# Moving a conditioning gate's row sums out of the seam between attention and output projection, and pacing an MLP between half products

## The chip, the cores and the metric

One core of a Trainium2 chip runs the whole program. The metric is the device time of one execution in microseconds. The kernel before took 890.24 us (median of 3 runs, 889.83 to 891.96). All matrix products run on TensorE (PE). VectorE (DVE), ScalarE (ACT) and GpSimd (POOL) do the elementwise work, and SyncE (SP) issues nearly all transfers.

## The reference

One decoder layer for 1024 tokens and a model width of 1024. All of this is computed in float32:

- `mod = c @ w_ada + b_ada` gives a shift, a scale and a gate of 1024 numbers each, from one conditioning vector `c`.
- `h = rms_norm(x) * (1 + scale) + shift`, and `proj = h @ w_in` gives queries, keys, values, SiLU gate paths (z) and merge gates.
- Mixer A is sparse attention with 8 heads in 2 groups: a compressed branch, whose keys and values come from blocks of 32 tokens through a small MLP (2048 to 256 to 64), a branch over selected blocks, and a window of 512. Mixer B is attention over a window of 128, with sinks, also 8 heads in 2 groups.
- Both outputs are multiplied with `silu(z)`, projected, merged with `sigmoid(m_a)` and `sigmoid(m_b)`, and multiplied by `w_out`.
- The result is `x + gate * rms_norm(y)`. The gate is the last third of `mod`, and nothing needs it before this last line.

With 16 blocks of 64 tokens and 16 to select, every causal block is selected, so the kernel does that branch as full causal attention.

## The kernel before

**Precision.** Each product of two float32 matrices is made from a high and a low part of each operand: high by high, high by low and low by high, three matmuls into the same PSUM bank. So every weight block is first *split*: a copy to the high type on ACT (L179, or L175 on DVE for two of them, or L177) and a subtraction on POOL (L182). Activations are split on ACT and DVE.

**Stages, in order of time in the profile.**

1. Up to about 60 us: `mod` for shift and scale (multiply-and-reduce on DVE over rows of `w_adaT`, L290), the norm, h for the first half of the tokens, and the first products.
2. About 60 to 166 us: h for the second half of the tokens, the values' products, and then two things in parallel: the products for six gate blocks Z (`z_halves`, lines 588 to 593, each block in two halves of the tokens, 24 matmuls of 512 columns each), and the compression MLP (`mlp`, lines 641 to 696), once for keys (side 0) and once for values (side 1). The MLP loads eight slices of `w1` per side, splits each on ACT (L653) and DVE (L654) and multiplies it in six matmuls of 256 columns (L657 to L659). POOL meanwhile forms sums of h (`input_sums`, from line 724), tied to marks among the Z products (`z_marks`). These sums are for a fast matrix product (seven half-size products in place of eight) that computes most of the merge gates.
3. About 166 to 696 us: four attention units, (B,0), (B,1), (A,0) and (A,1). Each goes over 8 blocks of 128 queries. For each head: scores on PE (L864, L867), adding the distances and taking the minimum on DVE (L874), the exponential on ACT (L887), the scale on POOL (L896), a transpose on PE (L933), its split on ACT and DVE (L939, L940), and the products with the values (L941, L944). Between these, projections fill PE (`b_pj`, L205 to L213 in the first two units, L1004 to L1010 in the last two).
4. About 691 to 809 us, the seam and the output: the last parts of the fast merge gate product (L1341 to L1345), loading the heads' outputs back and splitting them (`heads_out`, L1325 to L1327), the projections of the heads (`gated`, L1401 to L1403), and sums of `w_out` rows for the fast product with `w_out`.
5. To the end: that product (L1531 to L1536), norm, gate and addition.

**What sets the order.** The program is traced in Python, and a planner then puts every engine's instructions in an order: it simulates a timeline, takes the instruction with the highest priority of those that are ready, and takes tile buffers from a free pool. Each engine runs its own queue in that order, and SP's queue holds nearly all transfers. `tc.high_priority(offset=n)` moves a block forward or, with a negative offset, back. `after(a, b)` and `chain(tag, a)` add a dependency without a semaphore: it orders the plan, and between instructions of one engine it orders their queue. The clock of the plan inside the units is `done[0]`, which counts attention columns only: `mark` appends a score or transpose matmul to `marks`, `held(at)` returns the matmul that was there at that time, and `AHEAD = 3` is how much earlier than its place a thing may go. `pieces` is a list of (time, function); `pump` calls those that are due, at low priority. In the units before the change, only (A,0) and (A,1) use it.

**Places that the change touches.**

- Gate rows. `gate_load` (from line 1352) loads 8 row blocks of `w_adaT` of 128x1024, 512 KB each, in the seam, and L1374 loads `c` broadcast to all 128 rows. `gate_sum` (from line 1357) multiplies and reduces on DVE, L1359. They use the places of the heads' tiles `oh0` to `oh3`, `ol0` and `ol1`.
- Key fronts. `k_block` puts 64 columns of compressed keys ahead of each half of the keys of the selected branch, L543 (high) and L544 (low), on DVE, into a tile of the tag `kts`.
- `set_form` (L1058 to L1063) splits the sums of h for the fast product, a copy on ACT and a subtraction on POOL, when a projection piece begins (`Part.piece`). There `hold[0] = held(at - AHEAD)` stood after the call that triggers these copies.

The tag `kts` has 8 buffers, which the MLP's `w1` parts, the key tiles and the sums of weight quarters (`paced_sums`) share.

## Time and profile before

| What | Value |
|---|---|
| Median of 3 runs | 890.24 us |
| The profiled execution | 895.18 us |
| Span of that execution, first to last instruction | 893.3 us |
| Granted TensorE clock, mean | 0.988 |
| Busy: PE, DVE, ACT, POOL | 868.8, 630.2, 534.1, 532.7 us |
| Moved by DMA | 151.46 MB, 170 GB/s mean |

"Busy" counts the time in which an engine executes an instruction. Matmuls overlap in a pipeline: a 512-column matmul is listed with some 0.39 us, but in a full stream a new one starts each 0.23 us. So a busy PE can still be slow, and the number of matmuls in a stretch says more than its busy time. A row of the groups of instructions is: line, engine, operation, the tile written and the tiles read, shapes, count, then times. In a row of the timeline, the bracket at the end is how long the engine had been idle and what ended that. The granted clock is the share of full speed that the throttle let TensorE have.

### The profile page before, as it was taken

What the parts mean: (1) busy time and instruction counts of PE and PEld (TensorE: products, weight loads), DVE (VectorE), ACT (ScalarE), POOL (GpSimd) and SP (SyncE); (2) the same over time, 40 slices, a digit from 0 to 9 for tenths busy, and PEclk for the clock granted to TensorE, in tenths of its full rate; (3) what the DMA queues carried; (4) which work ended last, traced back from release to release, by engine and by line L of the source; (5) the groups of instructions that cost most, each with busy time, mean ns of one, the idle gap of its engine ahead of it and who ended that gap; (6) DMA issues with size and microseconds to landing.
All of it is one profiled execution on the core that took longest, in us unless ns stands there. A gap on an engine that the chain in (4) does not pass through costs nothing.

```text
span 893.3 us, 14739 instructions
## 1 busy us (share of the span) xinstructions
PE 868.8 (97%) x4418; PEld 730.1 (82%) x4418; DVE 630.2 (71%) x1579; ACT 534.1 (60%) x1210; POOL 532.7 (60%) x547
## 2 busy tenths in 40 slices
PE   8999999999999999999999999999999989999996
PEld 6989878888888887878888878888887868887885
DVE  4866775465666577667666677677675499998996
ACT  6466742276777777647657786666565435544341
POOL 1000966867867888866637686654573349855541
PEclk7999999999999999999999999999999989999998
DMA  9875565854534554643333334333553698951323
GB/s 349 282 271 181 178 202 189 287 163 152 180 110 133 171 152 159 212 147 94 99 109 101 89 107 131 107 121 103 163 174 101 243 387 275 331 157 49 107 94 118
DMA packets 92001, 151.46 MB, mean 170 GB/s; under 512 B 10769, under 2 KB 28561, under 8 KB 91922
## 3 DMA queue, kind: packets, MB, share of 16 engines
q1 hardware_dynamic: 90768, 149.30, 50.9%
q10 hardware_dynamic: 1154, 1.23, 0.5%
q8 instruction: 35, 0.57, 0.3%
q14 instruction: 44, 0.36, 0.1%
HBM read 108.81 MB, written 38.01 MB: 164 GB/s over the span
## 4 chain that ended last, share of the span: by engine, by line
PE 82%; DMA 5%; DVE 4%; issue 3%; ACT 2%; POOL 2%; SPq 1%; DVEq 0%; POOLq 0%; ACTq 0%
PE b_pt L933 7%; PE b_pj L1004 6%; PE b_pj L1010 6%; PE b_pj L1009 6%; PE b_pv L944 4%; PE b_s L867 4%; PE b_pj L212 4%; PE b_pj L213 4%; PE b_pj L205 4%; PE b_s L864 4%; PE b_pv L941 4%; DMA wg<-in_w_adaT 2%; PE b_s L228 1%; PE b_s L229 1%; DVE w L654 1%
## 5 line engine op out<-in xcount | busy, mean ns | idle before, releaser
L182 POOL TENSOR_TENSOR wl<-wraw,wh 128x512 fp32r<-128x512 f32 x123 | 167.0, 1361 | 80.7 <-ACT wh L179 61.4
L940 DVE TENSOR_TENSOR pl<-b_pt,ph 128x512 fp32r<-128x512 f32 x162 | 110.6, 687 | 44.0 <-ACT ph L939 41.2
L939 ACT CAST ph<-b_pt 128x512 fp32r<-128x512 f32 x162 | 93.4, 584 | 56.2 <-PE b_pt L933 50.2
L887 ACT ACTIVATE ps<-ps,mins 128x257 f32<-128x257 f32 (+9 forms) x128 | 81.3, 636 | 34.8 <-DVE mins L874 32.4
L179 ACT CAST wh<-wraw 128x512 fp32r<-128x512 f32 x115 | 70.6, 618 | 50.1 <-PE b_pj L1009 19.7
L864 PE MATMUL b_s<-kh,q 128*128 128x256 f32 (+6 forms) x272 | 85.6, 321 | 2.2 <-DVE mins L874 1.7
L867 PE MATMUL b_s<-kl,q 128*128 128x256 f32 (+6 forms) x272 | 83.5, 314 | 0.0
L1004 PE MATMUL b_pj<-hh,wh 128*128 128x512 f32 x188 | 77.7, 413 | 0.0
L896 POOL TENSOR_SCALAR ps<-ps,rr,gates 128x128 f32<-128x128 f32 (+7 forms) x64 | 52.5, 824 | 41.3 <-DVE rr L891 22.2
L1010 PE MATMUL b_pj<-hh,wl 128*128 128x512 f32 x188 | 74.5, 396 | 0.0
L1009 PE MATMUL b_pj<-hl,wh 128*128 128x512 f32 x188 | 74.0, 393 | 0.0
L944 PE MATMUL b_pv<-pl,V 128*128 128x512 f32 x162 | 68.3, 422 | 1.4 <-DVE pl L940 1.2
L941 PE MATMUL b_pv<-ph,V 128*128 128x512 f32 x162 | 67.0, 413 | 2.2 <-DVE ot L958 1.5
L933 PE MATMUL b_pt<-ident,ps 128*128 128x128 f32 x408 | 67.0, 272 | 0.1
L205 PE MATMUL b_pj<-hh,wh 128*128 128x512 f32 x160 | 63.1, 394 | 0.0
L213 PE MATMUL b_pj<-hh,wl 128*128 128x512 f32 x160 | 63.0, 394 | 0.0
L212 PE MATMUL b_pj<-hl,wh 128*128 128x512 f32 x160 | 62.9, 393 | 0.0
L864 PEld LDWEIGHTS b_s<-kh,q 128*128 128x128 f32 x272 | 51.2, 188 | 10.6 <-DVE mins L874 2.6
L933 PEld LDWEIGHTS b_pt<-ident,ps 128*128 128x128 f32 x408 | 51.1, 140 | 10.0 <-DVE pl L940 0.5
L896 POOL TENSOR_SCALAR pw<-pw,rr,gates 128x640 f32<-128x640 f32 (+4 forms) x64 | 47.4, 745 | 19.4 <-DVE rr L891 17.1
L867 PEld LDWEIGHTS b_s<-kl,q 128*128 128x128 f32 x272 | 51.1, 189 | 7.4
L887 ACT ACTIVATE pw<-pw,mins 128x640 f32<-128x640 f32 (+4 forms) x64 | 44.5, 695 | 18.0 <-DVE mins L874 17.8
(453 smaller groups left out, 2502.8 us busy)
## 6 DMA issues: line engine op xcount, KB each, us to landing
wraw<-in_w_blk SPq DMA_DIRECT2D x83, 256.0 KB, 3.2
r<-in_w_out SPq DMA_DIRECT2D x32, 256.0 KB, 5.0
wa<-in_w_adaT SPq DMA_DIRECT2D x15, 512.0 KB, 5.1
wraw<-sS SPq DMA_DIRECT2D x28, 256.0 KB, 2.9
w1raw<-in_w SPq DMA_DIRECT2D x16, 256.0 KB, 4.1
wraw<-in_w_o SPq DMA_DIRECT2D x16, 256.0 KB, 5.0
t<-od SPq DMA_DIRECT2D x16, 256.0 KB, 5.8
wg<-in_w_adaT SPq DMA_DIRECT2D x8, 512.0 KB, 7.0
```

The source lines that it names most:

```text
L182: chain("wl", nc.gpsimd.tensor_tensor(wl, raw, wh.bitcast(F32), ALU.subtract))
L864: ins = nc.tensor.matmul(sp[:, :n_in], lhsT=q, rhs=rh, start=True, stop=False)
L867: nc.tensor.matmul(sp[:, :n_in], lhsT=q, rhs=rl, start=False, stop=True)
L887: nc.scalar.activation(rows[r][:, :on], rows[r][:, :on], AF.Exp, scale=-1.0, bias=last_min[:, r : r + 1], accum_out=sums[:, r : r + 1])
L896: nc.gpsimd.tensor_scalar(rows[r][:, :off], rows[r][:, :off], rr[:, r : r + 1], gate, ALU.mult, ALU.mult)
L933: ins = nc.tensor.transpose(t[:, r * P : r * P + P], rows[r][:, off : off + P], ident)
L940: nc.vector.tensor_tensor(pl, t, ph.bitcast(F32), ALU.subtract)
L941: ins = nc.tensor.matmul(pv, lhsT=v, rhs=ph, start=(first and n == 0), stop=False)
L944: nc.tensor.matmul(pv, lhsT=v, rhs=pl, start=False, stop=(last and n == len(todo) - 1))
L1004: ins = nc.tensor.matmul(self.t, lhsT=wh[:, kc, :], rhs=hi, start=(self.first is None and kc == 0), stop=False)
L1009: nc.tensor.matmul(self.t, lhsT=wh[:, kc, :], rhs=lo, start=False, stop=False)
L1010: ins = nc.tensor.matmul(self.t, lhsT=wl[:, kc, :], rhs=hi, start=False, stop=(kc == KH - 1 and self.stop))
```

## The change

Four edits:

1. **Gate sums.** The loads and sums for the gate leave the seam. Each of the 8 row blocks is halved by columns. Half 0 of all is loaded and summed in unit (B,0), half 1 in unit (B,1), which adds to the first half's partial sum. The halves go through single `kts` buffers (128x512), their half of `c` through a tile of the tag `zt` or `ot`, which the first two units do not use. Loads stand at shares 0.08 + 0.11 k of the unit and sums at 0.14 + 0.11 k, by `pieces`.
2. **MLP between half products.** `z_halves` becomes `z_steps`, which stops in the middle of each product (after 4 of 8 row blocks, 12 matmuls) and at its end. Three steps come before the MLP. Within each side of the MLP, one step follows each of the first seven `w1` slices, at a priority 500 lower, and the first matmul of each next slice is tied behind it. The remaining steps come after. A block's successor is loaded after its first half, and `z_marks` are now the middles of the products.
3. **Key fronts.** The two copies in `k_block` go from DVE to ACT.
4. **Splits tied to half products.** `hold[0]` is set before what begins with a piece, the copies of `set_form` are tied behind `hold[0]`, and the loads of `paced_sums` behind `held` of their own time.

```diff
             elif pre:
-                nc.vector.tensor_copy(khp[:, pre - 64 : pre], kc2[:, 0, keys[r][1], :].bitcast(F32))
-                nc.vector.tensor_copy(klp[:, pre - 64 : pre], kc2[:, 1, keys[r][1], :].bitcast(F32))
+                nc.scalar.copy(khp[:, pre - 64 : pre], kc2[:, 0, keys[r][1], :].bitcast(F32))
+                nc.scalar.copy(klp[:, pre - 64 : pre], kc2[:, 1, keys[r][1], :].bitcast(F32))
...
-    def z_halves(names):
-        for name in names:
-            w = load_block(name)
+    def z_steps(names):
+        w = load_block(names[0])
+        for n, name in enumerate(names):
             for half in range(2):
-                z_block(name, half, w)
-                yield
+                t = bank(("s", "pj")[z_count[0] % 2])
+                for kc in range(KC):
+                    wh, wl = (x[:, kc % KH, :] for x in w[kc // KH])
+                    ins = nc.tensor.matmul(t, lhsT=wh, rhs=hh[kc][half], start=(kc == 0), stop=False)
+                    if kc == 0:
+                        chain("pj", ins)
+                    nc.tensor.matmul(t, lhsT=wh, rhs=hl[kc][half], start=False, stop=False)
+                    ins = nc.tensor.matmul(t, lhsT=wl, rhs=hh[kc][half], start=False, stop=(kc == KC - 1))
+                    if kc == 3:
+                        yield ins
+                z_out(name, half, t)
+                if half == 0 and n + 1 < len(names):
+                    following = load_block(names[n + 1])
+                yield ins
+            w = following
...
-                    nc.tensor.matmul(t[:, :256], lhsT=fh[:, l, :], rhs=h, start=(l == 0), stop=False)
+                    ins = nc.tensor.matmul(t[:, :256], lhsT=fh[:, l, :], rhs=h, start=(l == 0), stop=False)
+                    if n and l == 2 * n:
+                        after(ins, z_done[-1])
...
+                if n < 7:
+                    with tc.high_priority(offset=-500):
+                        z_done.append(next(zs))
...
-        zs = z_halves([f"Z{m}{b}" for m, b in (("B", 0), ("B", 1), ("B", 2), ("B", 3), ("A", 0), ("A", 1))])
+        zs = z_steps([f"Z{m}{b}" for m, b in (("B", 0), ("B", 1), ("B", 2), ("B", 3), ("A", 0), ("A", 1))])
+        z_done = []
+        for _ in range(3):
+            z_done.append(next(zs))
         with tc.high_priority(offset=500):
             blocks_of(0)
             mlp(0)
             blocks_of(1)
             mlp(1)
-        z_marks = []
-        for _ in zs:
-            z_marks.append(last["pj"])
+        z_done += list(zs)
+        z_marks = z_done[::2]
...
+                hold[0] = held(at - AHEAD)
                 if self.before:
                     self.before()
...
-            nc.scalar.copy(hi, lo.bitcast(F32))
+            after(nc.scalar.copy(hi, lo.bitcast(F32)), hold[0])
...
+    gate_c, gate_part = [None], sm.tile([P, 8], F32, name="gpart")
+
+    def gate_half(h):
+        gate_c[0] = at.tile([P, HS], F32, name="cg", tag=("zt", "ot")[h], bufs=1)
+        nc.sync.dma_start(gate_c[0], io["c"][h * HS : h * HS + HS].partition_broadcast(P))
+
+    def gate_sum(k, h):
+
+        blk, part, was = 16 + k, gate_part[:, k : k + 1], []
+
+        def get(when):
+            was.append(kq.tile([P, P + HS], F32, name="wg", tag="kts", bufs=8)[:, :HS])
+            after(nc.sync.dma_start(was[0], io["w_adaT"][blk * P : blk * P + P, h * HS : h * HS + HS]), held(when))
+
+        def add(when):
+            wa = was[0]
+            after(nc.vector.tensor_tensor_reduce(
+                out=wa, in0=wa, in1=gate_c[0], scale=1.0, scalar=part if h else smalls[:, 8 + blk : 9 + blk],
+                op0=ALU.mult, op1=ALU.add, accum_out=mod[:, blk : blk + 1] if h else part), held(when))
+
+        return get, add
...
+            gate_half(u)
+            for k in range(8):
+                for f, share in zip(gate_sum(k, u), (0.08, 0.14)):
+                    pieces.append((begun + whole[u] * (share + 0.11 * k), f))
+            pieces.sort(key=lambda x: x[0])
...
-        gate_c = op.tile([P, S], F32, name="cg", tag="oh0")
-        places = ["oh1", "oh2", "oh3", "ol0", "ol1"]
-        owing = []
-
-        def gate_load(k):
-            wa = op.tile([P, S], F32, name="wg", tag=places[k % 5])
-            nc.sync.dma_start(wa, io["w_adaT"][(16 + k) * P : (17 + k) * P, :])
-            owing.append((16 + k, wa))
-
-        def gate_sum():
-            blk, wa = owing.pop(0)
-            nc.vector.tensor_tensor_reduce(
-                out=wa, in0=wa, in1=gate_c, scale=1.0, scalar=smalls[:, 8 + blk : 9 + blk],
-                op0=ALU.mult, op1=ALU.add, accum_out=mod[:, blk : blk + 1])
...
-            if n == 0:
-                nc.sync.dma_start(gate_c, io["c"].partition_broadcast(P))
-            gate_load(2 * n)
-            gate_load(2 * n + 1)
...
-            if n:
-                gate_sum()
...
-        while owing:
-            gate_sum()
```

More of the change, by code (lines that the diff above doesn't have):

```diff
@@ L557, in k_fills @@
         return [lambda: k_block([("slc", g), ("win", g)], half, load_block(f"KA{g}"))]
-    def z_block(name, half, w):
-        z_out(name, half, proj_half(w, half, lambda: bank(("s", "pj")[z_count[0] % 2])))
     z_count = [0]
@@ L575, in z_out @@
         nc.sync.dma_start(spilled[name][:, half * HS : half * HS + HS], sp)
-    def z_fills(mixer, g):
-        res = []
-        for p in range(2):
-            def block(name=f"Z{mixer}{2 * g + p}"):
-                w = load_block(name)
-                for half in range(2):
-                    z_block(name, half, w)
-            res.append(block)
-        return res
-    def z_halves(names):
-        for name in names:
-            w = load_block(name)
-            for half in range(2):
-                z_block(name, half, w)
-                yield
+    def z_steps(names):
+        w = load_block(names[0])
+        for n, name in enumerate(names):
+            for half in range(2):
+                t = bank(("s", "pj")[z_count[0] % 2])
[13 more added lines that the diff above has]
+            w = following
     spilled = {}
@@ L1179, in paced_sums @@
         quads = {}
-        def get():
+        def get(when):
             a11, a12 = (kq.tile([P, HS], F32, name="sa", tag="kts", bufs=8) for _ in range(2))
@@ L1185, in get @@
             for n, t in ((2, a21), (3, a22), (0, a11), (1, a12)):
-                nc.sync.dma_start(t.rearrange("p (k t) -> p k t", k=KH), quarter_of(PAIRS[p][n // 2], n % 2))
-        return get, lambda: pair_sums(p, *quads[0])
+                after(nc.sync.dma_start(t.rearrange("p (k t) -> p k t", k=KH), quarter_of(PAIRS[p][n // 2], n % 2)),
+                      held(when))
+        return get, lambda when: pair_sums(p, *quads[0])
+    gate_c, gate_part = [None], sm.tile([P, 8], F32, name="gpart")
[4 more added lines that the diff above has]
+        blk, part, was = 16 + k, gate_part[:, k : k + 1], []
+        def get(when):
+            was.append(kq.tile([P, P + HS], F32, name="wg", tag="kts", bufs=8)[:, :HS])
[6 more added lines that the diff above has]
+        return get, add
     late = []
@@ L1241, in hybrid_kernel @@
                     ahead_of(line[k - 2], lambda k=k: set_form("T2", (k,)))
-                def paced(share, f):
-                    pieces.append((begun + whole[u] * share, lambda at: f()))
                 for n, p in enumerate(range(FIRST, NP)):
                     for f, share in zip(paced_sums(p), (0.18, 0.23)):
-                        paced(share + 0.09 * n, f)
+                        pieces.append((begun + whole[u] * (share + 0.09 * n), f))
             else:
@@ L1385, in hybrid_kernel @@
             nc.scalar.activation(y, y, AF.Sigmoid)
-            if n:
-                gate_sum()
             early[b, 1], early[b, 0] = e, y
-        while owing:
-            gate_sum()
         nc.vector.tensor_tensor(amod, mod[:, 16:24], g_post, ALU.mult)
```

## The prediction

> **What bounds the kernel now.** I read first the page's busy times and its chain of waits, to see which engine sets the end:
>
> ```profile
> span 893.3 us, 14739 instructions
> PE 868.8 (97%) x4418; PEld 730.1 (82%) x4418; DVE 630.2 (71%) x1579; ACT 534.1 (60%) x1210; POOL 532.7 (60%) x547
> ...
> PE 82%; DMA 5%; DVE 4%; issue 3%; ACT 2%; POOL 2%; SPq 1%; DVEq 0%; POOLq 0%; ACTq 0%
> PE b_pt L933 7%; PE b_pj L1004 6%; PE b_pj L1010 6%; PE b_pj L1009 6%; PE b_pv L944 4%; PE b_s L867 4%; PE b_pj L212 4%; PE b_pj L213 4%; PE b_pj L205 4%; PE b_s L864 4%; PE b_pv L941 4%; DMA wg<-in_w_adaT 2%; PE b_s L228 1%; PE b_s L229 1%; DVE w L654 1%
> ```
>
> TensorE is idle for only 893.3 - 868.8 = 24.5 us, so a gain can come only from that idle time and from slow matmuls. The change adds and removes no matmul. Yet two things that the change moves stand in the chain by name: wg, the gate rows' load (2% is some 18 us), and w L654, the low half of the compression MLP's weights. Where the idle time lies, the busy times by stretch show (columns: length, PE, PEld, DVE, ACT, POOL busy with instruction counts, granted clock, DMA share, GB/s):
>
> ```profile
> 100.00:125.00 25.00, 22.78 (x119) 18.66 (x118) 20.12 (x17) 15.35 (x22) 19.07 (x13) 1.00 0.59 190
> 725.00:750.00 25.00, 21.46 (x79) 16.52 (x79) 24.39 (x26) 12.39 (x23) 19.42 (x14) 0.86 0.89 311
> 750.00:775.00 25.00, 25.00 (x111) 20.57 (x110) 21.14 (x23) 14.27 (x27) 22.31 (x15) 1.00 0.96 325
> 875.00:893.30 18.30, 10.44 (x58) 8.95 (x56) 11.84 (x24) 2.97 (x10) 1.41 (x2) 0.86 0.27 100
> ```
>
> The tail's 7.9 us is not touched. The worst stretch in reach is 725 to 750: 79 matmuls where the next stretch has 111, DVE busy 24.39 of 25, the clock down to 0.86. At 25 / 111 = 0.225 us each, 32 missing matmuls are 7.2 us. What TensorE waits for, over the whole run (total us, times, longest):
>
> ```profile
> PE b_pt L658 <- DVE w L654: 2.6, 4, 0.7
> PE b_pt L1401 <- ACT oh L1326: 1.8, 1, 1.8
> ...
> PE b_s L864 <- DVE mins L874: 1.7, 1, 1.7
> PE b_pv L941 <- DVE ot L958: 1.5, 2, 1.1
> PE b_pv L944 <- DVE pl L940: 1.2, 4, 0.5
> PE b_pt L1401 <- ACT wh L179: 1.1, 1, 1.1
> ...
> PE b_pt L1402 <- DVE ol L1327: 0.6, 1, 0.6
> ```
>
> So there are three places: the MLP (L658), one stall in the attention (L864), and the seam between attention and output (the L1401 and L1402 rows).
>
> **Part 1, the gate sums leave the seam.** Around 710 the DMA engines are full, and after the first stall the clock is halved:
>
> ```profile
> 710.00:715.00 5.00, 5.00 (x24) 4.14 (x23) 5.00 (x9) 2.50 (x4) 0.00 (x0) 1.00 1.05 415
> ...
> 730.00:735.00 5.00, 5.00 (x14) 3.84 (x14) 4.42 (x7) 1.14 (x2) 3.72 (x3) 0.55 1.03 395
> ```
>
> ```profile
> 727.05 0.50 PE L1401 MATMUL b_pt<-oh,wh 128*128 128x512 f32 x1 [1.83 <-ACT oh L1326]
> ...
> 728.78 0.80 PE L1402 MATMUL b_pt<-ol,wh 128*128 128x512 f32 x1 [0.59 <-DVE ol L1327]
> ...
> 729.80 0.63 PE L1402 MATMUL b_s<-ol,wh 128*128 128x512 f32 x1
> ...
> 734.06 0.60 PE L1403 MATMUL b_pv<-oh,wl 128*128 128x512 f32 x1
> ```
>
> From 729.80 to 734.06 there are ten steps of 0.426 us, 0.20 more than 0.225: idle 1.83 + 0.59 + 1.12 = 3.5 us and slow matmuls 14 x 0.20 = 2.8 us, with the refill of the pipeline after each gap (some 0.2 us each) 7.0 us, which agrees with 7.2 by counting. The transfers behind it:
>
> ```profile
> t<-od SPq DMA_DIRECT2D x16, 256.0 KB, 5.8
> wg<-in_w_adaT SPq DMA_DIRECT2D x8, 512.0 KB, 7.0
> ```
>
> ```profile
> wraw<-in_w_blk SPq DMA_DIRECT2D x83, 256.0 KB, 3.2
> ...
> L1359 DVE CUSTOM_DVE_ANT_0 wg<-wg,cg,smalls x8: 1272/1280/2023, 709.7 to 737.0; 128x1024 f32<-128x1024 f32 x8
> ```
>
> Eight loads of 0.52 MB and the broadcast of c to 128 rows of 4 KB, 4.7 MB in all, are 11.7 us of transfer at about 400 GB/s. They stand on SP's queue between the heads' loads (t), which take 5.8 us to land where a load of the same size takes 3.2 us elsewhere. The first stall waits for such a head. With the gate loads gone the heads' backlog goes, and DVE loses 10.8 us of sums (8 x 1.28, one at 2.02) in the stage where it is full. What is late next: DVE's head splits and the w_out sums, now with 11 us of room between 705 and 760. I take back 6.3 of the 7.0 us, leaving one pipeline gap of 0.7; bounds 7.2 (all) and 3.0 (the clock's 2.8 us and the 0.2 of its refill only, idle stays).
>
> In the Trainium skill, "TensorE: Matmul & The Clock Gate", Part 1, an idle window of about 3.4 us halves the clock. The trace halves it after 1.83 us with 0.59 us behind it, and doesn't at the 1.7 us stall of L864 (clock 1.00, row below). By the page as by these rows, a single short stall that stays would not bring the slow 2.8 us back.
>
> **Part 2, the gate sums enter the first two units.** They become 16 loads of 256 KB, 2 broadcasts of 256 KB and 16 sums of 128x512. The nearest rows for such a sum: the same kind of instruction on 512 columns, and subtractions with both inputs in SBUF beside a busy POOL (min/median/max ns):
>
> ```profile
> L874 DVE CUSTOM_DVE_ANT_0 ps<-b_s,DC 128x512 f32<-128x512 f32 x32 | 21.7, 687 | 5.9 <-PE b_pt L933 4.4 <-PE b_s L867 1.2
> ...
> L654 DVE TENSOR_TENSOR w<-w1raw,w x16: 679/1252/1792, 86.2 to 145.0; 128x512 fp32r<-128x512 f32 x16
> ```
>
> So 0.69 to 1.79 us each, 11 to 29 us in all. What hides them (a sum over 166 to 310, then the low parts of the probabilities and the products that read them, 175 to 310; the loads that mark the two units; the transfers of 160 to 320):
>
> ```profile
> sum 144.00, PE 144.00 PEld 122.48 DVE 87.27 ACT 101.33 POOL 109.03; mean PE 20.57 PEld 17.50 DVE 12.47 ACT 14.48 POOL 15.58
> ```
>
> ```profile
> L940 DVE TENSOR_TENSOR pl<-b_pt,ph x31: 671/685/692, 180.9 to 304.3; 128x512 fp32r<-128x512 f32 x31
> ...
> L944 PE MATMUL b_pv<-pl,V x31: 388/393/483, 185.8 to 306.5; 128*128 128x512 f32 x31
> ```
>
> ```profile
> L955 SPq DMA_DIRECT2D zb<-sp_ZB x32: 592/600/673, 162.0 to 295.0; - x32
> ```
>
> ```profile
> DMA packets 21011, 26.48 MB, mean 166 GB/s; under 512 B 2398, under 2 KB 11358, under 8 KB 20995
> ```
>
> DVE is free for 144 - 87.3 = 57 us there and TensorE never waits. Pairing the 31 low parts with their products in order, the first is ready 4.2 us ahead (180.9 + 0.69 to 185.8), the last, already in the third unit, 1.5 us; of the others none is under 3.1 us. A sum of up to 1.8 us fits under that. Behind each sum on DVE stand score minima and low parts, and TensorE waits for those; behind each load on SP stand weights and spilled tiles, for which nothing waited here. 4.7 MB over the two units' 133 us is 35 GB/s on top of 166, where the seam moved 400. I take 0; bounds -0.3 and +3 (two stalls of the size at L864).
>
> The skill's "SBUF — State Buffer", Who interferes with whom, speaks against this move: a DVE instruction with two SBUF inputs and a GpSimd one that reads SBUF shut each other out for a whole instruction. L654's 1792 ns and L1359's 2023 ns agree. By that rule 16 sums would be near 30 us instead of 11; both are under the 57 us and the 3.1 us of cover, so the sum stays.
>
> **Part 3, the MLP between half products.** Each pair of w1 slices (six matmuls of 0.12 us) now comes after a half of a gate product (twelve of 0.225, 2.7 us). DVE's split, up to 1.79 us, has 3.4 us, so the 2.6 us wait goes. What it adds is alternating. The 256-column matmul ahead of a 512-column one held TensorE for 0.22 us in one place and 0.12 in another:
>
> ```profile
> 112.60 0.38 PE L657 MATMUL b_pt<-w,fh 128*128 128x256 f32 x1
> 112.82 0.40 PE L205 MATMUL b_s<-hh,wh 128*128 128x512 f32 x1
> ```
>
> ```profile
> 142.32 0.28 PE L657 MATMUL b_pt<-w,fh 128*128 128x256 f32 x1
> 142.44 0.40 PE L205 MATMUL b_s<-hh,wh 128*128 128x512 f32 x1
> ```
>
> Some ten more alternations than now: 0 to 1.0 us; I take 0.5, the middle. Net -2.1; bounds -2.6 and +1 (one new wait of 1 to 2 us when the second MLP starts and its flat split is late). The next block's load is issued half a block earlier, and the marks for the sums of h move by some 1.5 us; their product is read 300 us later:
>
> ```profile
> L740 POOL TENSOR_TENSOR q<-hh,hl x8: 1282/1292/3316, 94.4 to 157.9; 128x512 f32<-128x512 f32 x8
> ...
> L1062 ACT CAST hht<-hlt x16: 606/620/627, 463.8 to 656.0; 128x512 fp32r<-128x512 f32 x16
> ```
>
> **Part 4, front copies and split ties.** One front copy is behind the 1.7 us stall at 399: DVE stood 3.23 us before it and then 2.21 us in it, with the score minima queued behind:
>
> ```profile
> 398.60 2.21 DVE L543 CAST kh<-kc 128x64 fp32r<-128x64 f32 x1 [3.23 <-POOL sa L718]
> ...
> 400.00:405.00 5.00, 3.74 (x18) 3.08 (x19) 3.38 (x14) 3.70 (x13) 3.23 (x7) 1.00 0.18 57
> ```
>
> On ScalarE the copy may wait for the same buffer, and then the exponentials and high parts stand behind it. I take half, -0.8; bounds -1.7 and +1.5 (the stall comes back on ACT). Tying the set splits to an earlier mark moves sixteen copies of 0.62 us on ACT within slack: 0, bounds -0.7 and +0.7.
>
> **The sum.** The profiled execution took 895.18 us (span 893.3 and 1.9 around it). -6.3 + 0 - 2.1 - 0.8 = -9.2, so 886.0 us for an execution like it. The median of the runs is 890.24, 4.9 us under the profiled one; the same difference gives 881.0 us. The costs' bounds taken together where most of them are independent give 877 to 885 for this case.
>
> **The rivals.**
> *The seam refills* (0.15). Its stall is not the gate loads' but DVE's and the heads' own: three t buffers, and DVE at 24.39 of 25. For it: the 1.1 us stall waits for a weight split behind w_out sums on DVE. Against: 11 of its busy us are the gate sums. Only 3.0 of 7.0 come back: 881.0 + 3.3 = 884.3.
> *The order in the third and fourth unit gets worse* (0.10). The order is planned anew, and cover is thin there: L864, L941 and L944 wait 1.7 + 1.5 + 1.2 = 4.4 us now. Twice that, and Part 4's gain gone: 881.0 + 4.4 + 0.8 = 886.2. Against: those units get no new work but four pairs of short copies.
> *The half-product order doesn't hold the pairs apart* (0.08): a tie orders the plan, and the splits still come late, 881.0 + 2.1 = 883.1. Against: both are TensorE's, one queue.
> *Slower: each gate sum stops DVE's queue in the first two units* (0.07), waiting for its transfer and for POOL. DVE runs in order, so a block of b us costs 16 x (b - 4.3) once it is over the typical lead, 4.3 us (the pairs above lie between 3.1 and 5.8, but for the last); at b = 5.3, 16 us, so 897. It decides from the point where a load lands 3 us after its plan. For it: 256 KB take 3.2 us to land, and a load stands only 0.06 of a unit (133 / 2 x 0.06 = 4 us) ahead of its sum. Against: being 3 us late needs a landing of 7 us, seen only in the full seam.
>
> **How the numbers follow.** The forecast has 0.60, 877 to 885. Faster or slower by 0.3% (2.7 us) is about what a measurement can tell from no change. Faster (under 887.6): nearly all of the forecast, 0.59, of the seam rival 0.13, of the order rival 0.06, of the MLP rival 0.07, together 0.85; same 0.08, mostly the order rival; slower 0.07. The range 875.5 to 888 takes in the first three rivals and the bounds, and leaves out the slower one and the tails.
>
> **What would show it.** No wg row after 700; 725 to 750 shifted forward with 110 matmuls per 25 us and clock 1.00; t landing near 4 us. L658 without its wait on w. No TensorE wait between 175 and 300, and gate sums of 0.7 to 1.8 us there. The stall at L864 gone or under 1 us, without a new one behind ACT kh. I am wrong if waits on ps, pl or mins appear in the first two units, or if TensorE still stops for oh at the seam.

## The result and the profile after

The changed kernel took 895.04 us (median of 5 runs, 893.19 to 897.33), the kernel before 890.24. The ratio is 1.0053, with a 95% interval of 1.003 to 1.0076: slower by about half a per cent, where 881.0 was forecast. The profiled execution took 896.8 us. Its page begins with the same TensorE time as before:

```profile
span 895.0 us, 14786 instructions
...
PE 870.6 (97%) x4418; PEld 732.0 (82%) x4418; DVE 624.2 (70%) x1587; ACT 534.3 (60%) x1218; POOL 535.9 (60%) x547
...
PE b_pj L1010 7%; PE b_pj L1016 7%; PE b_pj L1015 7%; PE b_pt L938 6%; PE b_pv L949 4%; PE b_s L872 3%; PE b_s L869 3%; PE b_pv L946 3%; POOL hlw L1429 2%; POOL wl L182 1%; PE b_s L1542 1%; PE b_s L1540 1%; PE b_s L1537 1%; PE b_pv L921 1%; POOL wt L1429 1%
```

Both names that the change was to take off the chain, wg and the low half of the MLP's weights, are gone from it, but the time is not shorter. The busy times by stretch show where it went (columns as before). After the change:

```profile
100.00:125.00 25.00, 24.68 (x129) 20.85 (x128) 17.87 (x16) 13.46 (x21) 20.15 (x13) 1.00 0.58 199
...
175.00:200.00 25.00, 20.69 (x90) 16.31 (x89) 8.08 (x30) 10.27 (x29) 9.16 (x11) 0.86 0.71 221
200.00:225.00 25.00, 21.44 (x111) 17.71 (x109) 16.84 (x49) 14.78 (x43) 20.46 (x26) 0.93 0.58 184
225.00:250.00 25.00, 23.76 (x131) 19.86 (x132) 18.71 (x58) 18.33 (x55) 19.55 (x24) 1.00 0.64 190
...
725.00:750.00 25.00, 25.00 (x112) 20.68 (x111) 23.74 (x22) 15.28 (x29) 25.00 (x17) 1.00 0.88 297
```

The same stretches of the two first units before, which the prediction had not shown because nothing waited there:

```profile
175.00:200.00 25.00, 25.00 (x133) 21.25 (x132) 15.58 (x40) 17.26 (x46) 16.20 (x21) 1.00 0.55 171
200.00:225.00 25.00, 25.00 (x135) 21.26 (x134) 14.42 (x43) 17.56 (x48) 18.98 (x24) 1.00 0.53 164
225.00:250.00 25.00, 25.00 (x137) 21.27 (x135) 15.27 (x45) 18.60 (x53) 22.75 (x27) 1.00 0.55 172
```

From 100 to 125 us TensorE is now nearly gapless, and from 725 to 750 it does 112 matmuls in place of 79, at full clock. Both gains came. Between 175 and 225 us it does 201 matmuls in place of 268, with the clock down to 0.86 and 0.93. What TensorE waits for, over the run after:

```profile
PE b_s L869 <- DVE mins L879: 6.0, 4, 2.6
PE b_pt L938 <- POOL ps L901: 2.5, 1, 2.5
PE b_pv L949 <- DVE pl L945: 1.8, 4, 1.1
...
PE b_pt L938 <- DVE pl L945: 1.2, 3, 0.8
```

These are waits on mins, ps and pl, most of them in the first two units (of the 6.0 us on mins, 1.1 stand at 319 us, behind them): what the prediction named as the sign that it is wrong.

To add up slow matmuls and gaps together I use one measure below, the *excess*: the time from each matmul's start to the next one's, less its time in a full stream (0.227 us for 512 columns, in proportion for fewer, 0.085 for a transposition), summed over a stretch. It is good to some 2 us over a whole run.

| Excess, us | before | after | change |
|---|---|---|---|
| MLPs, 100 to 150 | 5.5 | 1.6 | -3.9 |
| first two units, 150 to 300 | 6.8 | 22.4 | +15.6 |
| last two units, 300 to 675 | 31.6 | 26.6 | -5.0 |
| seam, 675 to 775 | 9.7 | 3.2 | -6.5 |

So 15.4 us came and 15.6 went. The two profiled executions lie 1.6 us apart (895.18 and 896.8), the medians 4.8: the profiled execution before was itself 4.9 us above its median, the one after 1.8. A difference between two profiles can therefore be some 3 us off from the difference of the medians. Two places hold most of the 15.6. The first is the start of the first unit (timeline after):

```profile
177.48 0.67 PE L689 MATMUL b_pt<-w2v,h1T 128*63 128x64 f32 x8
...
179.10 0.49 DVE L699 TENSOR_TENSOR vc<-vcf,vc 128x128 fp32r<-128x128 f32 x2
...
179.55 0.34 ACTq L760 DMA_DIRECT2D DC<-in_DC  x1
...
186.35 0.35 DVE L879 CUSTOM_DVE_ANT_0 ps<-b_s,DC,nsink 128x128 f32<-128x128 f32 x1 [3.84 <-DMA DC<-in_DC]
...
186.77 0.33 PE L869 MATMUL b_s<-kh,q 128*128 128x128 f32 x1 [1.82 <-DVE mins L879]
...
190.65 0.47 PE L938 MATMUL b_pt<-ident,ps 128*128 128x128 f32 x1 [2.49 <-POOL ps L901]
...
191.35 0.63 PE L212 MATMUL b_pj<-hl,wh 128*128 128x512 f32 x1
```

The second MLP's last product (w2v) stands at 177.48 us. Then the load of the distance table DC is issued, it takes 6.8 us to land (3.7 before), and only then can the first row of scores be reduced. Before the change the same three steps were:

```profile
160.29 0.33 ACTq L755 DMA_DIRECT2D DC<-in_DC  x1
...
161.08 0.67 PE L686 MATMUL b_pt<-w2v,h1T 128*63 128x64 f32 x8
...
166.94 0.35 DVE L874 CUSTOM_DVE_ANT_0 ps<-b_s,DC,nsink 128x128 f32<-128x128 f32 x1
```

The paced MLP ends 16.4 us later, the table's load starts 19 us later, and TensorE, which had gate products to do until then, has nothing left. The second place is a gate sum (timeline after):

```profile
205.75 0.59 SPq L1209 DMA_DIRECT2D wg<-in_w_adaT  x1
...
209.24 1.77 DVE L1213 CUSTOM_DVE_ANT_0 wg<-wg,cg,smalls 128x512 f32<-128x512 f32 x1 [1.10 <-DMA wg<-in_w_adaT]
...
211.48 0.38 PE L869 MATMUL b_s<-kh,q 128*128 128x256 f32 x1 [2.64 <-DVE mins L879]
...
213.08 0.63 PE L946 MATMUL b_pv<-ph,V 128*128 128x512 f32 x1
```

DVE stands 1.10 us for the load, sums for 1.77 us, and the score minima behind it come 2.64 us too late. Over the run the sums wait for their loads seven times:

```profile
L1213 DVE CUSTOM_DVE_ANT_0 wg<-wg,cg,smalls x8: 739/750/1767, 202.1 to 243.2; 128x512 f32<-128x512 f32 x8
...
  DMA wg<-in_w_adaT: 9.8, 7
```

### The profile page after: what moved, and what is told of

Read it like the earlier page. It is cut to its first block, busy times and chain, and to the rows that moved or that the text cites. A ratio compares the mean times of both kernels' runs of the same rounds, so it can differ in the third digit from the quotient of the medians.

```text
span 895.0 us, 14786 instructions
## 1 busy us (share of the span) xinstructions
PE 870.6 (97%) x4418; PEld 732.0 (82%) x4418; DVE 624.2 (70%) x1587; ACT 534.3 (60%) x1218; POOL 535.9 (60%) x547
## 4 chain that ended last, share of the span: by engine, by line
PE 50%; POOL 4%; issue 3%; DMA 2%; DVE 2%; ACT 1%; SPq 0%; DVEq 0%; POOLq 0%; ACTq 0%
PE b_pj L1010 7%; PE b_pj L1016 7%; PE b_pj L1015 7%; PE b_pt L938 6%; PE b_pv L949 4%; PE b_s L872 3%; PE b_s L869 3%; PE b_pv L946 3%; POOL hlw L1429 2%; POOL wl L182 1%; PE b_s L1542 1%; PE b_s L1540 1%; PE b_s L1537 1%; PE b_pv L921 1%; POOL wt L1429 1%
## 5 line engine op out<-in xcount | busy, mean ns | idle before, releaser
L1010 PE MATMUL b_pj<-hh,wh 128*128 128x512 f32 x188 | 77.4, 412 | 0.0
L1016 PE MATMUL b_pj<-hh,wl 128*128 128x512 f32 x188 | 74.2, 395 | 0.0
L1015 PE MATMUL b_pj<-hl,wh 128*128 128x512 f32 x188 | 73.9, 393 | 0.0
L896 DVE RECIPROCAL rr<-sums 128x1 f32<-128x1 f32 x192 | 28.1, 158 | 27.9 <-ACT pw L892 13.7
L205 PE MATMUL b_pj<-hh,wh 128*128 128x512 f32 x112 | 45.5, 406 | 0.0
L212 PE MATMUL b_pj<-hl,wh 128*128 128x512 f32 x112 | 45.0, 402 | 0.0
```

The costliest lines, as they stand in the source:

```text
L1010: ins = nc.tensor.matmul(self.t, lhsT=wh[:, kc, :], rhs=hi, start=(self.first is None and kc == 0), stop=False)
L1015: nc.tensor.matmul(self.t, lhsT=wh[:, kc, :], rhs=lo, start=False, stop=False)
L1016: ins = nc.tensor.matmul(self.t, lhsT=wl[:, kc, :], rhs=hi, start=False, stop=(kc == KH - 1 and self.stop))
```

## The experiments

Each ratio is to the kernel before, run beside it on the same chip; the chips differ from group to group, so kernels of different groups are compared by their ratios. The "ties" are the two lines `if n and l == 2 * n: after(ins, z_done[-1])`, which put each MLP block behind a half product.

### Taking the parts apart

Four kernels, each the kernel before with some of the four edits:

```
e1_no_mlp     front copies + ties of the splits + gate sums      (MLPs as before)
e2_no_gate    front copies + ties of the splits + paced MLPs     (gate sums in the seam)
e3_gate_only  gate sums
e4_mlp_only   paced MLPs
```

> The changed kernel with the MLP left in its old place (ahead of whole gate products); the gate sums, front copies and ties stay. In the changed kernel TensorE's excess over back-to-back matmuls grew by 15.5 us between 150 and 300, and fell by 3.9 at the MLP, 7.2 at the seam and 4.9 in the last two units. Theory 1 (the paced MLP ends 17 us later, so the first unit starts behind it; all 15.5 are its): 890.2 - 7.2 - 4.9 = 878. Theory 2 (the gate sums stop DVE's queue while they wait for their loads; all 15.5 are theirs): 890.2 + 15.5 - 7.2 - 4.9 = 894. Both, about 9 and 6 us: 884, with the waits at the start of the first unit gone and the ones behind gate sums left.

> The changed kernel with the gate sums back in the seam; the MLP pacing, front copies and ties stay. Theory 1 (late MLP): 890.2 - 3.9 + 15.5 - 4.9 = 897, the stalls before 191 stay. Theory 2 (gate sums): 890.2 - 3.9 - 4.9 = 881, no wait between 175 and 300. Both: about 890, stalls before 191 stay, the ones at 208 to 228 go, and the seam's stalls and halved clock near 727 come back.

> The kernel before with the gate sums alone moved. Theory 1: 890.2 - 7.2 = 883, no wait in the first two units. Theory 2: 890.2 - 7.2 + 15.5 = 898. Both: 889. In each case the seam runs without stalls.

> The kernel before with the MLP pacing alone. Theory 1: 890.2 - 3.9 + 15.5 = 902, stalls at the start of the first unit. Theory 2: 890.2 - 3.9 = 886, no new stall. Both: 895.

| | median us | ratio | excess 150 to 300 | seam |
|---|---|---|---|---|
| no paced MLPs | 892.94 | 1.0012 (0.9989 to 1.0035) | 14.6 | 3.5 |
| no gate sums | 896.28 | 1.0045 (1.0026 to 1.0063) | 16.4 | 11.4 |
| gate sums alone | 896.39 | 1.0046 (1.0027 to 1.0066) | 13.1 | 3.6 |
| paced MLPs alone | 898.57 | 1.0083 (1.0054 to 1.0112) | 15.3 | 10.1 |

Each of the two costs 6 to 10 us of excess in the first two units without the other, so both causes are there, and neither theory alone holds. They do not add up in the time: with the MLPs paced, the gate sums add next to nothing (1.0053 for the whole change, 1.0045 without them). The kernel before took 892.53 us on this chip, 2.3 us more than the expectations start from. Less that, all four came 1 to 7 us above what was expected even for both together: each is dearer than I had set it.

### What a gate sum costs: waiting, length, or order

Based on the kernel without paced MLPs (892.94 us):

The first sums over 8 columns only, the second sums over the condition vector's tile and loads nothing, the third has a longer lead:

```diff
-                out=wa, in0=wa, in1=gate_c[0], scale=1.0, ...
+                out=wa[:, :8], in0=wa[:, :8], in1=gate_c[0][:, :8], scale=1.0, ...
```

```diff
-            after(nc.sync.dma_start(was[0], io["w_adaT"][blk * P : blk * P + P, h * HS : h * HS + HS]), held(when))
...
-                out=wa, in0=wa, in1=gate_c[0], scale=1.0, ...
+                out=wa, in0=gate_c[0], in1=gate_c[0], scale=1.0, ...
```

```diff
-                for f, share in zip(gate_sum(k, u), (0.08, 0.14)):
+                for f, share in zip(gate_sum(k, u), (0.02, 0.14)):
```

> The change without the paced MLPs (892.9 us), and each gate sum runs over 8 of its 512 columns, so that it still waits for its load but takes some 0.1 us of VectorE instead of 0.73 to 2.9 (most of the gate's sum is left out). Theory W (waiting): what costs is that VectorE's queue stands until the sum's load has landed; the stalls behind it at 250 to 320 us stay, 891 to 893 us. Theory D (duration): what costs is the sums' own time in VectorE's queue; 881 to 884 us. Theory O (order): the pieces change the planned order of the queues, whoever waits; 891 to 893 us here and in the next two.

> The same without the paced MLPs, with the 16 sums at full length over the condition vector's tile that is there already, and their loads left out (the gate's weights do not enter). Theory W: nothing to wait for, 881 to 884 us. Theory D: the sums' time is all there, 890 to 893 us. Theory O: 891 to 893 us.

> The same without the paced MLPs, all 16 loads and sums kept, but each load is tied to a mark 0.12 of a unit ahead of its sum instead of 0.06 (about 8 us instead of 4). Theory W: the loads have landed when the sums come up, the waits of VectorE on them fall from 7.8 us to under 1, and the time to 883 to 886 us. Theory D: 891 to 893 us. Theory O: 891 to 893 us.

Measured: 883.99 us (0.9917, 0.9895 to 0.9939), 884.14 us (0.9922, 0.9895 to 0.995) and 884.86 us (0.9922, 0.99 to 0.9944). Each of the three theories loses a run as it was put: the waits were all still there in the first (8.1 us, eight times), the length was all there in the second (24 us in 16 sums, up to 3.7 each), and a cost of any pieces, whoever waits, would have been there in all three.

The first run is no clean test, though. It was to cut the length and did not: sums over 8 columns, which take 0.20 us undisturbed, took up to 3.66 us beside GpSimd (last section), and the 16 of them 17.4 us, against 19.8 in the kernel that they are based on. Waits and time together were nearly as large there, in one place a wait of 0.77 us and a sum of 3.66 behind it without a stall of TensorE, and still it is as fast as the other two. The excess from 200 to 322 us, in which the stalls of these kernels stand, is 20.3 in the kernel without paced MLPs, 13.0, 8.5 and 10.3 in these three, and 7.1 with the gate sums in the seam (next section; the first figure and the 13.0 are from executions 3.6 and 2.6 us above their medians). So long sums without loads cost little, and loads taken away or placed earlier bring most of the loss back. That the price comes where a wait and a long sum meet and outlast what covers them, as at 209 us in the changed kernel, is argued and not shown. Several hundred of the 4418 matmuls also stand in another order in each of these kernels, and that the order of the first one was an unlucky one is a rival that no run tests.

With the loads 0.12 of a unit ahead the waits fall from 7.8 us to 3.4, where less than 1 was expected, while sums become no shorter:

```profile
L1208 DVE CUSTOM_DVE_ANT_0 wg<-wg,cg,gpart x8: 718/1260/5018, 243.3 to 289.1; 128x512 f32<-128x512 f32 x8
...
  DMA wg<-in_w_adaT: 3.4, 3
```

Excess from 150 to 300 falls from 14.6 to 8.3. This kernel, which has everything but the paced MLPs and loads the gate rows twice as far ahead, is faster than both kernels of this case. One more thing stays open: two stalls of the kernel without paced MLPs stood not behind a sum but behind rows whose buffers a store freed late (252 and 314 us, 1.71 and 1.99 us; DVE had stood 5.03 and 5.50 us for a store of quarter sums and one of head outputs). The first is gone here and the second is 1.5; how a load on SP's queue delays these stores was not taken apart.

### The ties of the splits and the front copies alone

> The front copies on ScalarE and the ties of the splits alone; gate sums in the seam and MLPs as before the change. If the quieter last two units (excess 26.8 us instead of 31.7 between 300 and 675 us) come from these ties: 886 to 888 us, the seam's stalls of 7 us still there. Rival (they come from the gate sums' move or from where the pieces fall by chance): 890 to 892 us, the stall of 1.6 us at 399 us still there.

Measured 886.69 us, 0.9948 (0.993 to 0.9965), as the first theory said. The excess of the last two units is 25.6 against 31.6 before, and the stretch behind the stall at 399 us is whole (135 matmuls, 123 before), while the seam keeps its own gaps (kernel with these edits alone):

```profile
400.00:425.00 25.00, 25.00 (x135) 21.29 (x135) 18.03 (x51) 17.40 (x34) 15.50 (x14) 1.00 0.30 85
700.00:725.00 25.00, 21.85 (x94) 17.11 (x92) 23.69 (x34) 11.00 (x19) 6.65 (x5) 1.00 1.04 410
```

The other kernels say the same: from 322 to 675 us the excess is 22.4 to 23.4 in all fifteen kernels with these two edits, and 26.5 to 28.5 in the three without. Which of the two small edits does it, the runs don't tell. Against this kernel, gate sums as the change has them cost 0.64% (1.0012 to 0.9948, some 6 us) although the seam gains; with the longer lead they gain 0.26%, 2 us, which their intervals do not separate from none.

### The table's load, and both causes mended

The distance table gets memory of its own, ahead of the MLPs' scratch; to make room, the MLPs' raw weights have 3 buffers in place of 5.

```diff
+    tb = attn_es.enter_context(tc.tile_pool(name="tb", bufs=1, reuse_waits="tile"))
+    DC = tb.tile([P, S], F32, name="DC")
...
+    after(nc.scalar.dma_start(DC, io["DC"]), last["act"])
     with tc.tile_pool(name="c1", bufs=1, reuse_waits="tile") as c1:
...
-                raw = c1.tile([P, HS], F32, name="w1raw", tag="w1raw", bufs=5)
+                raw = c1.tile([P, HS], F32, name="w1raw", tag="w1raw", bufs=3)
```

> The changed kernel whole, but the distance table DC has memory of its own and is loaded before the compression MLPs; to make room the MLP's raw weight tiles have 3 buffers instead of 5. Theory S (start): the first attention unit starts late because the table's load waits for the memory of the paced MLPs, and with the table there by 130 us the stalls of 1.82 and 2.49 us at 187 and 191 us and the half clock after them are gone; 175-225 us falls from about 13 us of excess to the 5 of the gate sums, and the time from 895 to 887 us. Rival M (the MLP's end itself): the unit's start is late whatever the table does, since its rows, query and key tiles wait for the same memory; the stall stays or moves by a few us, 893 to 895 us.

> The whole change with both causes mended: the distance table in memory of its own, loaded before the MLPs (3 raw weight tiles), and each gate load tied 0.12 of a unit ahead of its sum instead of 0.06. If the two causes add up: the changed kernel's 895 us less 3 (the table alone took it to 892) less 8 (the earlier loads took the kernel without paced MLPs from 893 to 885) is 884 us, and the MLPs' 4 us may show besides, 880 to 884. Rival (the paced MLPs' end, some 17 us later, costs in its own right, since the gate blocks' products that used to cover the first unit's start are spent): 886 to 889 us, with stalls before 200 us.

> The whole change with the gate loads alone moved ahead to 0.12 of a unit; the table's load as in the changed kernel. If the causes add up: 895 less 8, 887 us, with the stalls of 1.8 and 2.5 us at 187 to 191 us still there. Rival (the late start of the first unit is what brought the loads and sums into each other's way, so the loads' lead gains little while it stands): 891 to 895 us.

> No paced MLPs, the gate loads ahead, and the distance table in memory of its own with 3 raw weight tiles instead of 5: what the table's move does by itself where the MLP ends early. If the 6 us between the kernel with both causes mended (891) and the one without pacing (885) are the pacing's own: 884 to 886 us here. Rival (the fewer weight tiles or the early table are what costs): 888 to 891 us.

With the table there, the two stalls at the unit's start are gone, as Theory S had it, but not most of the loss: the excess from 175 to 225 us falls only from about 15 to about 13, where 5 was expected, and TensorE now stands 3.14 us at 207, behind a gate sum that waited 2.53 us for its load and took 2.29. The first minimum starts 0.4 us after the start of the MLP's last step, where it was 7.3 us in the changed kernel (179.10 to 186.35). The changed kernel with the early table:

```profile
180.90 0.49 DVE L703 TENSOR_TENSOR vc<-vcf,vc 128x128 fp32r<-128x128 f32 x2
181.30 0.34 DVE L881 CUSTOM_DVE_ANT_0 ps<-b_s,DC,nsink 128x128 f32<-128x128 f32 x1
```

Three of these and the kernel with the earlier loads make a square, all with the gate loads 0.12 of a unit ahead:

| ratio (interval), median us | no paced MLPs | paced MLPs |
|---|---|---|
| table as in the change | 0.9922 (0.99 to 0.9944), 884.86 | 1.0007 (0.999 to 1.0024), 892.97 |
| table early, 3 raw tiles | 0.9996 (0.9985 to 1.0006), 890.18 | 0.9998 (0.9983 to 1.0013), 891.13 |

(The changed kernel with the early table and its own gate loads: 891.93 us, 0.9999, 0.9982 to 1.0017.) With the late table pacing costs 8 us, with the early one 1 us, which the intervals don't tell from none. So most of the price of pacing goes when the table is early. But my repair costs 5 us of its own: with 3 raw tiles the unpaced MLPs wait more (excess 8.8 from 100 to 150 us against 5.0, and 11.2 against 8.3 from 150 to 300). The first two expectations did not foresee that; the rival of the last one (888 to 891) did. And it blurs the square: with the early table pacing still costs 5.5 us of excess from 150 to 300 us (16.7 against 11.2, where it is 22.7 against 8.3 with the late one), and this is hidden by the 5.8 us that it gains in MLPs which the repair made worse (3.0 against 8.8). By the excess the late table is thus some 9 of 14 us, and the rest is not the table's. Nor do the causes simply add: from the changed kernel (1.0053) to the earlier loads alone (1.0007) 4 us came back where 8 were expected, and the stalls of 2.3 and 2.2 us at the unit's start stayed, as the rival said.

### Which part of the pacing: the ties

Based on the whole change with the earlier loads (892.97 us):

The first paces only the MLP of the keys, the second sets half products between every second pair of blocks, the third keeps the half products and drops the ties:

```diff
-                    if n and l == 2 * n:
+                    if side == 0 and n and l == 2 * n:
...
-                if n < 7:
+                if side == 0 and n < 7:
```

```diff
-                    if n and l == 2 * n:
+                    if n and n % 2 == 0 and l == 2 * n:
...
-                if n < 7:
+                if n < 7 and n % 2:
```

```diff
-                    if n and l == 2 * n:
-                        after(ins, z_done[-1])
```

> As the one before, but only the first of the two MLPs (keys) is paced by half products, the second (values) runs as before the change. Three of the four waits of 0.5 to 0.7 us before the change were in the first. If the paced MLP costs through its late end: the end moves by about half as much, gate products are left to cover the first unit's start, and the time is 881 to 883 us, 2 to 4 below the kernel with no pacing (885). Rival (any pacing delays the table's load into the unit's start): 886 to 888 us.

> The whole change with the gate loads 0.12 of a unit ahead, but half products are set only between every second pair of the MLP's blocks, so that half as many are spent there. If the paced MLP costs by the time of its end (177 us for its last product, against 161 without pacing): the end comes at about 169 us, some 79 projection matmuls no longer all spent before the first row is there, and the time is 885 to 888 us, between 885 (no pacing) and 893 (full). Rival (whatever ties the MLP to half products costs the same): 891 to 893 us.

> As the whole change with the earlier gate loads, but without the ties: the half products are handed out between the MLP's blocks, and no product of the MLP is made to wait for the half product ahead of it. If the ties are what moves the MLP's end: it ends near 161 us as before the change and the time is 884 to 887 us. Rival (handing the gate blocks out as half products is enough to move it): 890 to 893 us.

| | w2v product at | first row's minima | excess 175 to 225 | median us, ratio |
|---|---|---|---|---|
| no pacing (earlier loads) | 160.7 | 166.7 | 2.1 | 884.86, 0.9922 (0.99 to 0.9944) |
| no ties | 161.0 | 163.6 | 2.3 | 883.51, 0.9929 (0.9908 to 0.995) |
| every second block | 175.8 | 183.0 | 11.0 | 897.44, 1.008 (1.0062 to 1.0098) |
| full pacing | 175.8 | 185.2 | 14.4 | 892.97, 1.0007 (0.999 to 1.0024) |
| first MLP only | 183.3 | 190.6 | 13.5 | 892.78, 1.0015 (1.0002 to 1.0028) |

My two forecasts for half the pacing were wrong, and both times came above their rivals too: half as many ties do not move the end half as far. The end stays at 176 us, or goes to 183. But the theory under them holds: where the MLP ends at 161, nothing is lost, and wherever it ends at 176 or later, 9 to 12 us of excess follow. In the worst stall of all, with only the first MLP paced, TensorE stands until one table load has landed (issued at 186.0 us, 4.6 us on its way):

```profile
190.99 0.47 PE L869 MATMUL b_s<-kh,q 128*128 128x128 f32 x1 [7.04 <-DVE mins L879]
```

Without the ties the MLP's waits are back too (2.1 us on the low parts, against none): the kernel then behaves as if unpaced. Its table load is issued at 152.1 us, 9 us ahead of the w2v product, where it stood 0.8 us ahead of it before the change and 2.1 us behind it in the changed kernel. So it is not that product itself which lets the load go; whether the scratch memory that becomes free or the load's place in ScalarE's queue holds it back, these runs don't separate. Why every second block costs 4 to 6 us more than full pacing is not explained; its profile shows the same kind of stalls.

### GpSimd's backlog

From the kernel with both causes mended, the first pair of quarter sums moved from the first unit to the second, and the third pair from the start of the second to its middle:

```diff
-            for p in ((0, 1), (2,))[u]:
-                at_step.setdefault(4 * (p % 2), []).append(lambda p=p: late_sums(p))
+            for p in ((1,), (0, 2))[u]:
+                at_step.setdefault((0, 4, 4)[p], []).append(lambda p=p: late_sums(p))
```

> The kernel with both causes mended (891), with the sums of weight quarters on GpSimd spread differently: the first pair's, which ran at 196 to 205 us between the row scalings of the first unit, are moved into the second unit. If what is left of the loss is GpSimd's backlog in a first unit that starts late: the excess of 6.6 us between 200 and 225 us falls to 3 or less and the time to 886 to 888 us. Rival (the gate products' cover is spent, whatever GpSimd does): 890 to 892 us.

Measured 888.94 us, 0.9984 (0.997 to 0.9999), against 891.13 (0.9998): 2 us less, with intervals that meet, and more than the 886 to 888 that were expected. The excess from 200 to 225 us fell from 6.6 to 2.8, as expected. But TensorE now stops for 3.23 us at 288, behind a gate sum that waited for nothing and still took 4.85 us, beside GpSimd:

```profile
280.85 4.85 DVE L1215 CUSTOM_DVE_ANT_0 wg<-wg,cg,gpart 128x512 f32<-128x512 f32 x1
```

### The better version

Two complete kernels are the fastest here and beat both of this case: the change without paced MLPs and with gate loads 0.12 of a unit ahead (884.86 us, ratio 0.9922), and the same with half products but no ties (883.51 us, 0.9929). Between them there is no difference that these runs can tell. Both keep the seam's gain and the quieter last units. The two small edits alone beat both as well (886.69 us, 0.9948).

## Why the prediction was wrong, point by point

**Part 1 was right.** -6.3 was forecast. By excess the seam gave 6.5 us, from 725 to 750 us 33 more matmuls run, the clock is 1.00, the heads' loads land in 4.3 us in place of 5.8. The rival that the seam refills is out.

**Part 2 failed at "I take 0".** The cover I counted was that of the low parts, 3.1 us or more ahead of their products. A sum is in DVE's queue together with everything else, so what it needs covered is its wait *plus* its length (1.10 and 1.77 us at 209, with a stall of 2.64 behind them), and score minima, projections' splits and row buffers stand behind it as well as low parts. I had a bound for the length (up to 1.8 us; it went to 2.1 in the changed kernel and to 5.0 in another) and gave the wait to a rival with 0.07. Measured, the gate sums cost 6 us net of what the seam gains (ratio 1.0012 with them, 0.9948 without). The row for it was there: a load takes 3.2 us to land and stands 4 us ahead, a margin of 0.8 us. In the changed kernel the loads that DVE waited for had been issued only 0.6 to 4.3 us before it was ready for their sums. That such places cost is what the trace shows; how much of the 6 us is theirs, and how much the order into which the plan then falls, stays open. The "slower" rival had the mechanism and nearly the time (897), but not the shape: not all 16 sums cost, only a few places do, and that its time comes near is luck, since the pacing has its own share in the loss. And its condition, a landing of 7 us, never came in the changed kernel; the loads landed in 3.5 us (median) and up to 5.0, but were issued late.

In the Trainium skill, "SBUF — State Buffer", Who interferes with whom, has a DVE instruction with two SBUF inputs and a GpSimd one that reads SBUF shut each other out for a whole instruction. The same sum took 0.72 to 5.02 us in these runs, so the traces agree that such sums are held up; 5.02 us is more than one instruction (last section). All 16 took 17.6 us in the changed kernel, between the prediction's 11 and 30. By itself this cost nothing in the kernel with 24 us of such sums and no loads (884.14 us), and one stall of 3.23 us in the last one.

**Part 3 was right in place and wrong in reach.** The 2.6 us of waits in the MLPs went, and the excess fell by 3.9. But I costed only the products that I looked at. 14 half products of 2.7 us now *must* stand before the MLP's last one: the MLP stage took 44.0 us before (103.4 to 147.4) and 61.0 after (103.1 to 164.1). What becomes late with its end, the distance table's load above all, I did not name, although the text asked what is late next for the sums of h. The gate products spent early had kept TensorE busy at the unit's start. This took back 8 us (884.86 us without pacing, 892.97 with it), twice what the waits gave.

**Part 4 was undersized.** -0.8 was forecast; by the run with these edits alone they bring 0.35 to 0.7%, 3 to 6 us, because not one stall but several in the last two units go. The rival that these units get worse is out.

**The half-product order** does hold the pairs apart, contrary to the third rival. It needs its ties for that, and the ties are what costs: without them, and with nothing else changed, 892.97 us become 883.51.

## What to carry to other kernels

Filler work that is spent earlier is missing later: before a stage is paced with it, look for what waits for that stage's end (memory it frees, loads into that memory) and what covered that time until now. Work put into an in-order queue needs cover for its wait and its length together, so tie its load far ahead before asking whether the length fits; here twice the lead took 892.94 us to 884.86. And a fix in one stage shows in its own stretch of the profile even when the total gets worse, so judge edits one at a time.

## What the hardware showed besides

A stall of TensorE has a second price. In the changed kernel the granted clock is 0.50 from 188.6 us, behind the stall of 1.82 us, to 195.4, past the one of 2.49 us. Behind the second, the 512-column matmuls start 0.43 us apart instead of 0.23, nine times from 191.35 to 195.19 us:

```profile
190.00:195.00 5.00, 4.35 (x11) 3.48 (x12) 2.12 (x8) 0.79 (x2) 1.41 (x4) 0.50 0.81 264
```

Over all runs here, between 100 and 790 us, 18 of the 19 stalls of 1.82 us or more had such slow matmuls within the next 6 us. Of the eleven between 1.59 and 1.79 us four had, and of those from 0.9 to 1.57 us three of 32. (A few of the long ones have another stall within those 6 us, so they are not independent cases.) So a stall of 2 us can cost some 4 (nine steps that are 0.2 us too long are 1.8 us more), and one of up to 1.5 us mostly costs little beside itself. The prediction held that a single short stall would not slow the matmuls; from about 1.8 us on, these counts say otherwise. In the Trainium skill, "TensorE: Matmul & The Clock Gate", Part 1, an idle window of about 3.4 us brings the clock down. The traces agree on the length: between 100 and 790 us every stretch at half the clock lasts 3.4, 6.8 or 10.2 us. But stalls of half that window are enough to bring one on. The page also has the window run on its own, regardless of the kernel; that would fit a band of stall lengths that sometimes do it and sometimes don't.

The length of a gate sum was a surprise as well. Its 4.85 to 5.02 us are not one GpSimd instruction's worth. GpSimd in the kernel with the quarter sums moved:

```profile
278.31 1.28 POOL L182 TENSOR_TENSOR wl<-wraw,wh 128x512 fp32r<-128x512 f32 x1
279.56 1.29 POOL L727 TENSOR_TENSOR ps<-ps 128x512 f32<-128x512 f32 x1
280.84 1.83 POOL L903 TENSOR_SCALAR ps<-ps,rr 128x256 f32<-128x256 f32 x4
282.65 1.27 POOL L966 TENSOR_TENSOR ob<-ob,zb 64x512 f32<-64x512 f32 x1
283.88 1.26 POOL L182 TENSOR_TENSOR wl<-wraw,wh 128x512 fp32r<-128x512 f32 x1
```

GpSimd works without a gap until 285.14, and the sum on DVE, begun at 280.85, ends at 285.70, 0.56 us later: it seems to have had to wait for the end of GpSimd's whole run, not of one instruction. The longest sum of the kernel with earlier loads shows the same: it ends at 248.29, 0.55 us after a run of GpSimd instructions without a gap that ends at 247.74. The sums over 8 columns show it most plainly, since they have next to no work of their own. Nine of the 16 took 0.20 to 0.30 us; the other seven took 0.90 to 3.66 us, and each of these ended 0.02 to 0.03 us after a GpSimd instruction did. The longest, and the last GpSimd instruction of the run beside it:

```profile
244.84 3.66 DVE L1208 CUSTOM_DVE_ANT_0 wg<-wg,cg,gpart 128x8 f32<-128x8 f32 x1 [0.77 <-DMA wg<-in_w_adaT]
247.18 1.29 POOL L718 TENSOR_TENSOR ps<-ps 128x512 f32<-128x512 f32 x1
```

That it is a shared access which keeps the sum waiting is argued from these places, not tried by itself.
